# Norming h early into a second buffer, adaLN sections on VectorE, and three smaller edits to a four-layer trunk

## The chip, the core and the metric

The kernel runs on one core of a Trainium2 chip. The metric is the time of one execution on the device, in microseconds (us). Five engines work side by side and each takes its own instructions in order: TensorE (products; its weight loads are a queue of their own), VectorE, ScalarE, GpSimd, and SyncE, which issues nearly all DMAs.

## The reference

One inference step of a trunk of DEPTH = 4 layers over 384 tokens (128 context, 256 latent) of width 1024, in float32. Layer i mixes tokens by i mod 3: a chunked gMLP (layers 0 and 3), a pooling mixer (1), grouped-query attention (2). A gated ConvFFN follows in every layer. Each sub-layer norms, shifts and scales by adaLN, and adds a gated residual:

```python
m = silu(cond) @ w_ada[i] + b_ada[i]            # six sections: sh1, sc1, gt1, sh2, sc2, gt2
h = rms_norm(x, g_mix[i]) * (1 + sc1) + sh1
x = x + gt1 * mixer(h)
h = rms_norm(x, g_ffn[i]) * (1 + sc2) + sh2
a, u = split(h @ w_ffn_in[i])                   # 2 x 2816 wide
a = conv3(a) * conv_w + conv_b                  # width 3, along the tokens
x = x + gt2 * ((gelu(a) * u) @ w_ffn_out[i])
```

Context and latent tokens have a condition each, so each adaLN section is 1024 numbers for two conditions. The pooling mixer projects h in four groups and multiplies by a fixed 384-token averaging matrix.

## The kernel before

Features lie on partitions (8 blocks of 128, index k or d) and the 384 tokens along the free axis. `self.x` holds the residual stream, `hh` and `hl` the high and low part of h, 386 columns (TE) each: the two last columns carry the shift of the two conditions. A float32 product is made of three fp32r products (`mm3`): high weight by high h, low weight by high h, high weight by low h.

Weights stream through in chunks of 128x1024 in a written-out order (`chunk_plan`). SyncE loads a chunk into one of five `wraw` buffers. `w_split` makes `whi` on ScalarE (L338) and `wlo` on VectorE (L345), and `w_get` keeps three chunks split ahead of the one in use; there are four buffers of each part. AdaLN sections are chunks of the same stream, eight a section. The table `ADA` names for each phase which sections it makes and how: "ad" by `ada_dve` on VectorE (L380, two multiply-and-sum instructions a chunk), "ap" by `ada_pe` on TensorE (L398, four small products). `weave` lays them between the phase's weight chunks, leaving out a number of chunks at its head and tail (`EDGES`). `w_split` runs each "ad" chunk as soon as the weight chunk before it has been split.

A sub-layer's start works without the norm. While the residual is written (`residual`, L453), `prep` writes x times the gain into `hh`, `hl` and adds up the squares on the way (`square`); the first products of the next sub-layer begin at once. `stats` sums the squares over partitions with products of ones (L521), `diag` and `spread` (L536) lay the reciprocal root out as `rbs`, and the products' results are multiplied by it afterwards.

In `ffn` this goes: four `fr` chunks make f = 0 and 1 (block columns of `a` and `u`) into four PSUM banks, then `fi` makes f = 2 to 21 with two chunks and 48 products each, in two of six banks `mm`, and the epilogue of block f - 1 is issued inside block f. `epi_a` multiplies `a` and `u` by `rbs` on VectorE (L657, L661); `epi_b` adds the shift into `ab` on ScalarE (L671), scales (L673), and adds the two neighbours on VectorE (`ct`, L675); `epi_c` takes GELU (L681) and multiplies (`gg`, L684); `split_act` makes `gh` (L567) and `gl` (L568). `fo` is the second projection, in `out_proj`. `stat_k` is the k of `fr` before which the sums are made. In `gmlp` the phases are `gv`, `gu`, `go`; in `pool` a product of two rows (L948) brings in the shift's column sums before the averaging products, and the residual follows (L955).

## Time and profile before

| | |
|---|---|
| time, median of 3 runs | 1789.53 us (1789.23 to 1791.93) |
| the profiled execution: its own time | 1789.65 us |
| its span, first to last instruction | 1787.8 us |
| TensorE busy | 1766.3 us, 99% |
| VectorE busy | 1387.9 us, 78% |
| ScalarE busy | 873.9 us, 49% |
| read from memory | 308.06 MB |

The rows below come from that one execution. Times in them are counted from the span's start. PE is TensorE, PEld its weight loads, DVE VectorE, ACT ScalarE, POOL GpSimd, SP SyncE. A matmul's end is modelled, and consecutive ones overlap, so spacing is read from starts.

### The profile page before, as it was taken

How to read it: one execution, taken by the hardware profiler on the slowest of the kernel's cores; microseconds unless marked ns; L12 is line 12 of the kernel's file. 1: busy time of each engine (PE TensorE's matmuls, PEld its weight loads, DVE VectorE, ACT ScalarE, POOL GpSimd, SP SyncE). 2: the span in 40 equal slices, each digit the busy share in tenths (PEclk: the TensorE clock that was granted, in tenths of full speed). 3: DMA queues.
4: the chain of work that ended last, by engine and by line, in shares of the span. 5: the costliest groups of instructions: out<-in, count | busy, mean ns of one | idle time of the engine just before them, and what ended most of it. 6: DMA issues, size and time to landing. Idle time of an engine off the chain costs nothing.

```text
span 1787.8 us, 26990 instructions
## 1 busy us (share of the span) xinstructions
PE 1766.3 (99%) x10326; PEld 1682.8 (94%) x10326; DVE 1387.9 (78%) x2456; ACT 873.9 (49%) x1556; POOL 1.8 (0%) x30
## 2 busy tenths in 40 slices
PE   7999999999999999999999999999999999999999
PEld 5799899999998999999778999999988999999999
DVE  5877689998876888797787788878775787888732
ACT  3634335555445555432568465553354443555531
POOL 0000000000000000000000000000000000000000
PEclk9999999999999999999999999999999999999999
DMA  9775565554653444466543444436645255444341
GB/s 328 283 238 179 211 218 176 177 176 168 208 201 122 146 163 175 148 234 228 177 148 131 139 156 159 165 118 214 204 170 196 96 175 177 142 153 143 123 150 57
DMA packets 87637, 311.65 MB, mean 174 GB/s; under 512 B 10450, under 2 KB 10962, under 8 KB 87252
## 3 DMA queue, kind: packets, MB, share of 16 engines
q1 hardware_dynamic: 87364, 309.92, 49.8%
q8 instruction: 81, 1.33, 0.3%
q14 instruction: 48, 0.39, 0.1%
q10 hardware_dynamic: 144, 0.01, 0.0%
HBM read 308.06 MB, written 1.84 MB: 173 GB/s over the span
## 4 chain that ended last, share of the span: by engine, by line
PE 84%; DVE 10%; ACT 3%; issue 2%; DMA 1%; SPq 0%; DVEq 0%; ACTq 0%
PE mm L638 65%; PE mm L762 6%; DVE junk L380 3%; DVE wlo L345 2%; ACT whi L338 1%; PE S L638 1%; PE mm L806 1%; DMA wraw<-wts 1%; DVE ct L675 1%; PE S L1035 1%; PE psa L398 1%; PE adaT L638 1%; PE mm L928 1%; PE psa L762 1%; PE adaT L762 1%
## 5 line engine op out<-in xcount | busy, mean ns | idle before, releaser
L345 DVE TENSOR_TENSOR wlo<-wraw,whi 128x1024 fp32r<-128x1024 f32 (+2 forms) x390 | 465.8, 1200 | 188.7 <-ACT whi L338 187.7
L338 ACT ACTIVATE whi<-wraw 128x1024 fp32r<-128x1024 f32 (+2 forms) x390 | 399.7, 1035 | 305.3 <-PE mm L638 189.1
L638 PE MATMUL mm<-hh,whi 128*128 128x386 f32 (+1 forms) x1664 | 426.6, 341 | 0.0
L638 PE MATMUL mm<-hh,wlo 128*128 128x386 f32 (+1 forms) x1664 | 423.9, 340 | 0.7 <-DVE wlo L345 0.2
L638 PE MATMUL mm<-hl,whi 128*128 128x386 f32 (+1 forms) x1664 | 421.3, 338 | 0.0
L380 DVE SCALAR_TENSOR_TENSOR junk<-wraw,condb 128x1024 bf16<-128x1024 f32 x272 | 332.2, 1221 | 7.6 <-ACT condb L1499 2.7
L638 PEld LDWEIGHTS mm<-hh,whi 128*128 128x128 f32 x1664 | 300.6, 188 | 4.8 <-issue 2.1
L638 PEld LDWEIGHTS mm<-hh,wlo 128*128 128x128 f32 x1664 | 303.1, 188 | 2.0 <-DVE wlo L345 1.9
L638 PEld LDWEIGHTS mm<-hl,whi 128*128 128x128 f32 x1664 | 303.3, 188 | 0.0
L638 PE MATMUL mm<-gh,wlo 128*128 128x384 f32 x704 | 193.6, 336 | 0.0
L638 PE MATMUL mm<-gl,whi 128*128 128x384 f32 x704 | 193.6, 336 | 0.0
L638 PE MATMUL mm<-gh,whi 128*128 128x384 f32 x704 | 193.6, 336 | 0.0
L681 ACT ACTIVATE ct<-ct 128x385 f32<-128x385 f32 x88 | 46.1, 527 | 178.2 <-DVE ct L675 178.1
L638 PEld LDWEIGHTS mm<-gl,whi 128*128 128x128 f32 x704 | 128.5, 188 | 0.0
L638 PEld LDWEIGHTS mm<-gh,wlo 128*128 128x128 f32 x704 | 128.5, 188 | 0.0
L638 PEld LDWEIGHTS mm<-gh,whi 128*128 128x128 f32 x704 | 128.4, 188 | 0.0
L675 DVE SCALAR_TENSOR_TENSOR ct<-ab,par,ct 128x385 f32<-128x385 f32 x176 | 109.1, 621 | 22.3 <-ACT ct L673 17.4
L684 DVE SCALAR_TENSOR_TENSOR gg<-u,mm,ct 128x128 f32<-128x128 f32 (+1 forms) x176 | 66.3, 419 | 49.1 <-ACT ct L681 49.1
L586 ACT ACTIVATE hh<-x,A 128x128 fp32r<-128x128 f32 x96 | 43.2, 457 | 104.9 <-DVE x L453 94.1
L671 ACT ACTIVATE ab<-a,be 128x128 f32<-128x128 f32 (+1 forms) x176 | 70.7, 450 | 2.6
L657 DVE TENSOR_TENSOR a<-mm,rbs 128x384 f32<-128x384 f32 x88 | 48.6, 552 | 20.5 <-PE mm L638 14.5
L673 ACT ACTIVATE ct<-ab,par 128x385 f32<-128x385 f32 x88 | 62.7, 712 | 3.4
(301 smaller groups left out, 1961.9 us busy)
## 6 DMA issues: line engine op xcount, KB each, us to landing
wraw<-wts SPq DMA_DIRECT2D x562, 512.0 KB, 3.3
wraw<-wts SPq DMA_DIRECT2D x12, 256.0 KB, 2.6
wraw<-wts SPq DMA_DIRECT2D x8, 384.0 KB, 4.1
x<-x SPq DMA_DIRECT2D x4, 384.0 KB, 4.3
mx<-mix SPq DMA_DIRECT2D x1, 1280.0 KB, 7.1
y<-x SPq DMA_DIRECT2D x3, 384.0 KB, 3.1
condb<-condb SPq DMA_DIRECT2D x1, 1024.0 KB, 8.6
ws<-a_w_s SPq DMA_DIRECT2D x2, 512.0 KB, 4.0
```

What stands on the lines that cost most here:

```text
L338: nc.scalar.activation(hi[:, :n], t[:, :n], AF.Copy)
L345: nc.vector.tensor_tensor(out=lo[:, :n], in0=t[:, :n], in1=hi[:, :n].bitcast(F32), op=ALU.subtract)
L380: nc.vector.scalar_tensor_tensor(out=self.junk.bitcast(BF16), in0=w, scalar=1.0, in1=self.condb[:, c, :], op0=ALU.mult, op1=ALU.mult, accu ...
L586: nc.scalar.activation(self.hh[:, d, t0:t1], self.x[:, d, t0:t1], AF.Copy, scale=A[:, d, c:c + 1])
L638: nc.tensor.matmul(o, w[:, c:c + nw], r, start=(first and p == 0), stop=(last and p == 2))
L657: nc.vector.tensor_tensor(out=a1, in0=pa[:, 0:T], in1=rbs, op=ALU.mult)
L671: nc.scalar.activation(ab[:, p0:p1], a1[:, t0:t1], AF.Identity, bias=be[:, c:c + 1])
L673: nc.scalar.activation(t, ab[:, 1:T + 2], AF.Identity, scale=cw[1], bias=cb)
L675: nc.vector.scalar_tensor_tensor(out=t, in0=ab[:, i:i + T + 1], scalar=cw[i], in1=t, op0=ALU.mult, op1=ALU.add)
L681: nc.scalar.activation(t, t, GELU)
L684: nc.vector.scalar_tensor_tensor(out=g[:, t0:t1], in0=u1[:, t0:t1], scalar=bu[:, c:c + 1], in1=t[:, t0 + c:t1 + c], op0=ALU.add, op1=ALU.mult)
L762: nc.tensor.matmul(ps[n][i], hs, w[p == 1][:, c:c + 512], start=(k == 0 and p == 0), stop=(k == 7 and p == 2))
```

## The change

The second half of `ffn` reads a finished h. `norm` (with `put_act`) makes all eight blocks of h, normed, scaled and shifted, in a second buffer with rows of 384 columns as soon as `rbs` is known, and blocks f = 3 to 21 are made from it. Their epilogue needs no multiplication by `rbs` and no shift: ScalarE copies `a` from PSUM, takes GELU per group of tokens, and VectorE multiplies with `u` in PSUM. The sums are made and spread earlier (`stat_k`). From f = 2 to 7 the epilogue runs two blocks behind, at f = 8 two blocks are caught up. The two buffers `hb[0]` and `hb[1]` take turns; the idle one also holds the last eight blocks of `gh`, `gl` (or `ga`, `gb`, or the attention's `qS`). The gMLP's `gu` reads such plain rows too. `PLAIN`, `FPAD` and the pool `const2` only place buffers.

Three adaLN sections go from "ap" to "ad" (layer 0's fourth, layer 1's first, layer 2's third), and `ADA` and `EDGES` lay all sections out anew. At the start, products of ones (`warm`) stand before the first weights, before the first sums and after the first section. `add_square` adds the last square to the sum, so that `stats` takes one part. In `pool` the two rows of column sums are split into high and low parts at partitions 0, 32 and 64, so that one fp32r product takes the place of a float32 one.

The diff without its blank lines and a few lines of the same kind:

```diff
+NR = 3
+NG = NF - 8
+PLAIN = (32, 0)
+FPAD = 88
...
 ADA = {
-    (0, "gv"): [("ad", 0, 2)],
-    (0, "gu"): [("ad", 0, 3), ("ap", 0, 4)],
-    (0, "go"): [("ad", 0, 5), ("ap", 1, 1)],
-    (0, "fi"): [("ad", 1, 2), ("ad", 1, 0), ("ad", 1, 4, 0, 3)],
-    (0, "fo"): [("ad", 1, 4, 3, 8), ("ad", 1, 3)],
-    (1, "fi"): [("ad", 1, 5), ("ad", 2, 1, 0, 5)],
-    (1, "fo"): [("ad", 2, 1, 5, 8), ("ad", 2, 0), ("ad", 2, 4)],
-    (2, "nm"): [("ap", 2, 3, 0, 6)],
-    (2, "qkv"): [("ap", 2, 3, 6, 8)],
-    (2, "at"): [("ap", 2, 2), ("ap", 2, 5)],
-    (2, "fi"): [("ad", 3, 1), ("ad", 3, 2, 0, 3)],
-    (2, "fo"): [("ad", 3, 0), ("ad", 3, 2, 3, 8)],
-    (3, "gv"): [("ad", 3, 4), ("ad", 3, 3, 0, 1)],
-    (3, "go"): [("ad", 3, 3, 1, 8)],
+    (0, "gv"): [("ad", 0, 4)],
+    (0, "gu"): [("ad", 0, 2), ("ad", 0, 3, 0, 2)],
+    (0, "go"): [("ad", 0, 3, 2, 8), ("ad", 0, 5, 0, 3)],
+    (0, "fi"): [("ad", 0, 5, 3, 8), ("ad", 1, 1), ("ad", 1, 2), ("ad", 1, 0, 0, 5)],
+    (0, "fo"): [("ad", 1, 0, 5, 8), ("ad", 1, 4), ("ad", 1, 3)],
+    (1, "fi"): [("ad", 1, 5), ("ad", 2, 1), ("ad", 2, 0)],
+    (1, "fo"): [("ad", 2, 4), ("ad", 2, 3)],
+    (2, "nm"): [("ap", 2, 2, 0, 6)],
+    (2, "qkv"): [("ap", 2, 2, 6, 8)],
+    (2, "at"): [("ap", 2, 5)],
+    (2, "fi"): [("ad", 3, 1), ("ad", 3, 2)],
+    (2, "fo"): [("ad", 3, 0), ("ad", 3, 4, 0, 4)],
+    (3, "gv"): [("ad", 3, 4, 4, 8), ("ad", 3, 3, 0, 4)],
+    (3, "go"): [("ad", 3, 3, 4, 8)],
     (3, "fi"): [("ad", 3, 5)],
 }
-EDGES = {(0, "gv"): (2, 1), (0, "go"): (5, 0), (3, "gv"): (5, 2), "fi": (0, 6), (3, "go"): (5, 2)}
+EDGES = {(0, "gv"): (2, 1), (0, "go"): (5, 0), (3, "gv"): (5, 2), "fi": (8, 4), (3, "go"): (5, 2)}
...
+WARM = (25, 3, 10)
...
+        self.const2 = pool("const2", 1)
...
+    def add_square(self, pr):
+        self.nc.vector.tensor_tensor(out=pr["acc"], in0=pr["acc"], in1=pr["sq"], op=ALU.add)
...
+    def put_act(self, k, A, rbs, hi, lo, sh):
+        nc = self.nc
+        t = self.tmp.tile([128, T], F32, tag="sq", name="nt")
+        nc.vector.tensor_tensor(out=t, in0=self.x[:, k, :], in1=rbs, op=ALU.mult)
+        for c, (t0, t1) in enumerate(GRPS):
+            nc.scalar.activation(t[:, t0:t1], t[:, t0:t1], AF.Identity, scale=A[:, k, c:c + 1], bias=sh[:, k, c:c + 1])
+        nc.scalar.activation(hi[:, k, :], t, AF.Copy)
+        return lambda: nc.vector.tensor_tensor(out=lo[:, k, :], in0=t, in1=hi[:, k, :].bitcast(F32), op=ALU.subtract)
...
+    def use(self, n):
+        self.cur = n
+        w = KD * TE
+        self.hh, self.hl = (self.hb[n][:, w * i:w * i + w].rearrange("p (k t) -> p k t", t=TE) for i in range(2))
+    def plain(self, n):
+        w, o = KD * T, PLAIN[n]
+        return [self.hb[n][:, w * i + o:w * i + w + o].rearrange("p (k t) -> p k t", t=T) for i in range(2)]
...
     def ffn(self, l, pr, follow, stat_k):
         nc = self.nc
         hh, hl = self.hh[:, :, 0:TE], self.hl[:, :, 0:TE]
+        nh, nl = self.plain(1 - self.cur)
+        tail = self.plain(self.cur)
         with self.tc.tile_pool(name=f"ffn{l}", bufs=1) as fp:
-            gh = fp.tile([128, NF, T], F32R, tag="gh", name="gh")
-            gl = fp.tile([128, NF, T], F32R, tag="gl", name="gl")
+            fp.tile([128, FPAD], F32, tag="pad", name="pad")
+            own = [fp.tile([128, NG, T], F32R, tag=n, name=n) for n in ("gh", "gl")]
+            gh, gl = ([own[i][:, f, :] if f < NG else tail[i][:, f - NG, :] for f in range(NF)] for i in range(2))
...
             def epi_a(f, pa, pu):
+                if f >= NR:
+                    return f, pa, None, pu, None
...
                     p0, p1 = pos[c]
-                    nc.scalar.activation(ab[:, p0:p1], a1[:, t0:t1], AF.Identity, bias=be[:, c:c + 1])
+                    if f < NR:
+                        nc.scalar.activation(ab[:, p0:p1], a1[:, t0:t1], AF.Identity, bias=be[:, c:c + 1])
+                    else:
+                        nc.scalar.activation(ab[:, p0:p1], a1[:, t0:t1], AF.Copy)
...
             def epi_c(st, t):
-                _, _, _, u1, bu = st
+                f, _, _, u, bu = st
+                g = self.tmp.tile([128, T], F32, tag="gg", name="gg")
+                if f >= NR:
+                    for c, (t0, t1) in enumerate(GRPS):
+                        nc.scalar.activation(g[:, t0:t1], t[:, t0 + c:t1 + c], GELU)
+                    nc.vector.tensor_tensor(out=g, in0=u, in1=g, op=ALU.mult)
+                    return g
                 nc.scalar.activation(t, t, GELU)
-                g = self.tmp.tile([128, T], F32, tag="gg", name="gg")
                 for c, (t0, t1) in enumerate(GRPS):
-                    nc.vector.scalar_tensor_tensor(out=g[:, t0:t1], in0=u1[:, t0:t1], scalar=bu[:, c:c + 1],
+                    nc.vector.scalar_tensor_tensor(out=g[:, t0:t1], in0=u[:, t0:t1], scalar=bu[:, c:c + 1],
                                                    in1=t[:, t0 + c:t1 + c], op0=ALU.add, op1=ALU.mult)
                 return g
+            sh = self.prm[:, l, 24:32, :]
+            to_norm = list(range(KD))
+            def norm(n):
+                ks, to_norm[:] = to_norm[:n], to_norm[n:]
+                for i in range(0, len(ks), 2):
+                    for lo in [self.put_act(k, pr["A"], rbs, nh, nl, sh) for k in ks[i:i + 2]]:
+                        lo()
+            self.add_square(pr)
             b = [self.bank()[:, :TE] for _ in range(4)]
+            R = None
             for kk in range(4):
                 w = self.w_get("fr")
                 for k2 in range(2):
                     k = 2 * kk + k2
                     if k == stat_k:
-                        R = self.diag(self.stats(pr["acc"], pr["sq"]))
+                        R = self.diag(self.stats(pr["acc"]))
+                    if k == stat_k + 2:
+                        nc.scalar.activation(rbs, self.spread(R), AF.Copy)
+                        R = None
                     self.mm3([(b[i], 512 * k2 + 128 * i) for i in range(4)], w, (hh[:, k, :], hl[:, k, :]),
                              k == 0, k == 7)
-            nc.scalar.activation(rbs, self.spread(R), AF.Copy)
+                    if k > stat_k + 1:
+                        norm(2)
+            if R is not None:
+                nc.scalar.activation(rbs, self.spread(R), AF.Copy)
+            norm(2)
             prev = [(0, b[0], b[1]), (1, b[2], b[3])]
             for f in range(2, NF):
-                pa, pu = self.bank()[:, :TE], self.bank()[:, :TE]
+                w0 = TE if f < NR else T
+                pa, pu = self.bank()[:, :w0], self.bank()[:, :w0]
+                now, prev = (prev, []) if f == 8 else (prev[:1], prev[1:])
                 for kk in range(2):
                     if kk == 0:
                         sts = []
-                        w = self.w_get("fi", mid=lambda: sts.extend([epi_a(*p) for p in prev]))
+                        w = self.w_get("fi", mid=lambda: sts.extend([epi_a(*p) for p in now]))
                         ts = [epi_b(st) for st in sts]
                     else:
                         gs = [epi_c(st, t) for st, t in zip(sts, ts)]
                         w = self.w_get("fi")
                         for st, g in zip(sts, gs):
-                            self.split_act(g, gh[:, st[0], :], gl[:, st[0], :])
+                            self.split_act(g, gh[st[0]], gl[st[0]])
+                    if f < NR:
+                        norm(3)
                     for k4 in range(4):
                         k = 4 * kk + k4
-                        self.mm3([(pa, 256 * k4), (pu, 256 * k4 + 128)], w, (hh[:, k, :], hl[:, k, :]), k == 0, k == 7)
-                prev = [(f, pa, pu)]
+                        r = (hh[:, k, :], hl[:, k, :]) if f < NR else (nh[:, k, :], nl[:, k, :])
+                        self.mm3([(pa, 256 * k4), (pu, 256 * k4 + 128)], w, r, k == 0, k == 7)
+                prev.append((f, pa, pu))
+            assert not to_norm and len(prev) == 1
             sts = []
             self.w_split(self.n_get + 2, lambda: sts.extend([epi_a(*p) for p in prev]))
             g = epi_c(sts[0], epi_b(sts[0]))
-            self.split_act(g, gh[:, NF - 1, :], gl[:, NF - 1, :])
+            self.split_act(g, gh[NF - 1], gl[NF - 1])
+            self.use(1 - self.cur)
             res, after = follow()
...
+        hb = self.cur if pr is None else 1 - self.cur
+        vh, vl = self.plain(hb)
+        tail = self.plain(1 - hb)
         with self.tc.tile_pool(name=f"gmlp{l}", bufs=1) as gp:
             v = gp.tile([128, 3, DG], F32, tag="v", name="v")
-            ga = gp.tile([128, 16, T], F32R, tag="ga", name="ga")
-            gb = gp.tile([128, 16, T], F32R, tag="gb", name="gb")
+            own = [gp.tile([128, 8, T], F32R, tag=n, name=n) for n in ("ga", "gb")]
+            ga, gb = ([own[i][:, c, :] if c < 8 else tail[i][:, c - 8, :] for c in range(16)] for i in range(2))
...
+                self.add_square(pr)
...
-                            R = self.diag(self.stats(pr["acc"], pr["sq"]))
+                            R = self.diag(self.stats(pr["acc"]))
...
-                b = [self.bank()[:, :te] for _ in range(2)]
+                b = [self.bank()[:, :T] for _ in range(2)]
...
-                                 (self.hh[:, k, 0:te], self.hl[:, k, 0:te]), k == 0, k == 7)
+                                 (vh[:, k, :], vl[:, k, :]), k == 0, k == 7)
...
+            self.use(hb)
...
+            msr = pp.tile([128, 4, T], F32R, tag="msr", name="msr")
+            ush = pp.tile([128, 4, 256], F32R, tag="ush", name="ush")
+            nc.gpsimd.memset(msr.bitcast(F32), 0.0)
+            nc.gpsimd.memset(ush.bitcast(F32), 0.0)
...
-                u = pp.tile([128, 4, 256], F32, tag="u", name="u", bufs=3)
+                u = pp.tile([128, 3, 256], F32, tag="u", name="u", bufs=3)
+                if g == 0:
+                    for q in (0, 32):
+                        nc.vector.tensor_copy(msr[q:q + 2], ms)
+                    nc.vector.tensor_tensor(out=msr[64:66], in0=ms, in1=msr[0:2].bitcast(F32), op=ALU.subtract)
                 for i in range(3):
                     nc.scalar.activation(u[:, i, :], ps[i // 2][:, 256 * (i % 2):256 * (i % 2) + 256], AF.Copy,
                                          scale=r[:, i:i + 1])
-                nc.vector.tensor_copy(u[0:2, 3, :], ps[1][0:2, 256:512])
+                for q in (0, 64):
+                    nc.vector.tensor_copy(ush[q:q + 2, g, :], ps[1][0:2, 256:512])
+                nc.vector.tensor_tensor(out=ush[32:34, g, :], in0=ps[1][0:2, 256:512], in1=ush[0:2, g, :].bitcast(F32),
+                                        op=ALU.subtract)
...
-                    nc.tensor.matmul(ps, u[0:2, 3, c], ms[:, g, :], start=True, stop=False, skip_group_check=True)
+                    nc.tensor.matmul(ps, ush[:, g, c], msr[:, g, :], start=True, stop=False, skip_group_check=True)
...
-            qS = ap.tile([128, NH, T], F32R, tag="qS", name="qS")
+            o = PLAIN[1 - self.cur]
+            qS = self.hb[1 - self.cur][:, o:o + NH * T].rearrange("p (h t) -> p h t", t=T)
...
-        self.hh = self.const.tile([128, KD, TE], F32R, name="hh")
-        self.hl = self.const.tile([128, KD, TE], F32R, name="hl")
-        self.par = self.const.tile([128, NPAR], F32, name="par")
+        self.hb = [self.const.tile([128, 2 * KD * TE], F32R, name=f"hb{i}") for i in range(2)]
+        self.use(0)
+        self.par = self.const2.tile([128, NPAR], F32, name="par")
...
+        nc.scalar.activation(self.tmp.tile([128, 1], F32, tag="dmy", name="dmy", bufs=1), self.ones[:, 0:1], AF.Silu)
+        spare = self.bank("spare")
+        def warm(n):
+            for _ in range(WARM[n]):
+                nc.tensor.matmul(spare[:, 0:128], self.ones, self.ones, start=True, stop=True)
+        warm(0)
...
+        def first_stats():
+            warm(1)
+            r.append(self.stats(acc))
+        a0_mm(0, first_stats)
+        warm(2)
...
-            pr = self.ffn(l, pr, follow, 7 if kind == 1 else 5)
+            pr = self.ffn(l, pr, follow, 6 if kind == 1 else 3)
```

## Rows read from the trace of the kernel before

**Rows 1.** The page, busy time of each engine, share, instructions.
```profile
PE 1766.3 (99%) x10326; PEld 1682.8 (94%) x10326; DVE 1387.9 (78%) x2456; ACT 873.9 (49%) x1556; POOL 1.8 (0%) x30
```

**Rows 2.** Windows, L638 alone: layer 1's `fi`, layer 0's `fo`; busy (instructions).
```profile
590.00:750.00 160.00, 160.00 (x906) 160.00 (x906) 1.00 0.46 161
...
450.00:530.00 80.00, 80.00 (x463) 80.00 (x462) 1.00 0.60 208
```

**Rows 3.** Timeline, VectorE, layer 0's `fi`: start, duration, instruction [idle].
```profile
319.08 1.23 DVE L345 TENSOR_TENSOR wlo<-wraw,whi 128x1024 fp32r<-128x1024 f32 x1 [0.19 <-ACT whi L338]
320.22 0.55 DVE L568 TENSOR_TENSOR gl<-gg,gh 128x384 fp32r<-128x384 f32 x1
320.69 0.55 DVE L657 TENSOR_TENSOR a<-mm,rbs 128x384 f32<-128x384 f32 x1
...
321.62 1.21 DVE L345 TENSOR_TENSOR wlo<-wraw,whi 128x1024 fp32r<-128x1024 f32 x1
322.76 1.22 DVE L380 SCALAR_TENSOR_TENSOR junk<-wraw,condb 128x1024 bf16<-128x1024 f32 x1
...
325.17 1.27 DVE L675 SCALAR_TENSOR_TENSOR ct<-ab,par,ct 128x385 f32<-128x385 f32 x2
327.03 0.76 DVE L684 SCALAR_TENSOR_TENSOR gg<-u,mm,ct 128x128 f32<-128x128 f32 x2 [0.59 <-ACT ct L681]
327.98 1.22 DVE L345 TENSOR_TENSOR wlo<-wraw,whi 128x1024 fp32r<-128x1024 f32 x1 [0.19 <-ACT whi L338]
```

**Rows 4.** Timeline of TensorE: its first wait in that phase.
```profile
391.79 0.62 PE L638 MATMUL mm<-hh,wlo 128*128 128x386 f32 x2 [0.23 <-DVE wlo L345]
```

**Rows 5.** Timeline of TensorE around one adaLN chunk in layer 0's `gu`.
```profile
124.55 0.51 PE L638 MATMUL mm<-hl,whi 128*128 128x384 f32 x2
124.99 0.64 PE L398 MATMUL psa<-wraw,cond 128*32 128x256 f32 x8
125.56 0.62 PE L638 MATMUL mm<-hh,whi 128*128 128x384 f32 x2
```

**Rows 6.** Timeline of TensorE in layer 2's `fr`: one pair of sums, the spread.
```profile
1020.66 0.36 PE L521 MATMUL cs<-ones,sq 128*128 128x1 f32 x2
...
1027.32 0.81 PE L536 MATMUL adaT<-R,ones 128*128 128x384 f32 x2
```

**Rows 7.** Timeline of TensorE: adaLN products of the start.
```profile
9.38 1.08 PE L1437 MATMUL psa<-wraw,cond 128*32 128x256 f32 x8 [9.38 <-DMA wraw<-wts]
...
20.18 1.07 PE L1437 MATMUL psa<-wraw,cond 128*32 128x256 f32 x16
```

**Rows 8.** Timeline of the pool: column sums on TensorE, residual on VectorE.
```profile
560.73 0.91 PE L948 MATMUL mm<-ms,u 2*128 2x384 f32 x2
...
562.85 0.91 PE L948 MATMUL mm<-ms,u 2*128 2x384 f32 x2
...
562.02 0.73 DVE L955 SCALAR_TENSOR_TENSOR x<-mm,pgs,x 128x128 f32<-128x128 f32 x2
...
564.22 0.74 DVE L955 SCALAR_TENSOR_TENSOR x<-mm,pgs,x 128x128 f32<-128x128 f32 x2
```

**Rows 9.** Timeline of ScalarE in layer 0's `fi`.
```profile
321.48 0.81 ACT L671 ACTIVATE ab<-a,be 128x128 f32<-128x128 f32 x2
...
326.47 0.53 ACT L681 ACTIVATE ct<-ct 128x385 f32<-128x385 f32 x1 [3.44 <-DVE ct L675]
326.90 1.04 ACT L338 ACTIVATE whi<-wraw 128x1024 fp32r<-128x1024 f32 x1
327.85 0.51 ACT L567 ACTIVATE gh<-gg 128x384 fp32r<-128x384 f32 x1
```

**Rows 10.** Timelines of ScalarE and VectorE after layer 2's spread.
```profile
1028.16 0.49 ACT L697 ACTIVATE rbs<-adaT 128x384 f32<-128x384 f32 x1 [3.77 <-PE adaT L536]
...
1035.24 1.42 DVE L684 SCALAR_TENSOR_TENSOR gg<-u,mm,ct 128x128 f32<-128x128 f32 x4 [0.49 <-ACT ct L681]
```

**Rows 11.** Windows, the span's end: us, busy of five engines, granted clock.
```profile
1786.00:1788.00 2.00, 0.00 (x0) 0.00 (x0) 0.00 (x0) 0.00 (x0) 0.00 (x0) 0.70 0.20 73
```

41 lines of the change are left out of this document (19 added, 22 removed).

## The prediction

> **What bounds the kernel now.** First the busy totals [rows 1]: TensorE 99% of the span, VectorE 78%, ScalarE 49%. A busy TensorE is not yet TensorE at its best, so second I read the spacing of the products by stage [rows 2]. In layer 1's `fi` phase 906 products of 386 columns begin or end in 160 us, one every 176.6 ns; in layer 0's `fo` phase 463 of 384 columns in 80 us, one every 172.8 ns. Between the two stands no wait: over most of the span TensorE is simply supplied without gaps, and what is taken from it comes off the time one for one, as long as the others keep pace.
>
> Third I looked for the stage where they don't: VectorE's timeline over one block f of layer 0's `fi` [rows 3]. From the `wlo` at 319.08 to the one at 327.98 are 8.90 us: two `wlo` of 1.14, `gl` 0.47, `a` and `u` 0.93, one adaLN chunk 2.41 (322.76 to 325.17), two `ct` with the wait for GELU 1.86 (1.27 of work, 0.59 of wait), `gg` with the wait for the next `whi` 0.95. TensorE needs 48 x 176.6 = 8.48 us for the same f. So VectorE falls 0.42 us behind at each f, and its queue runs in order: both waits stay unfilled though it is late. TensorE notices only at 391.79 [rows 4], some 13 f after the phase settled at about 283 us. That is 13 x 0.42 = 5.5 us of cover, which the three chunks split ahead and the six banks give; I use 6. From there to the phase's end at 444 TensorE runs at VectorE's pace, about 5 f x 0.42 = 2 us lost.
>
> **The change part by part: what TensorE saves.** Narrower products: from f = 3 on `fi` reads h from a buffer with rows of 384 instead of 386 columns: 19 f x 48 = 912 products in each of four FFNs at 3.8 ns less is 13.9 us. Whether width or row pitch makes the 3.8 isn't settled by these rows; lower bound 0. A further 672 products in the gMLP's `gu` phases lose the pitch: 0 to 2.6, I take 2. The Trainium skill (TensorE: Matmul & The Clock Gate, "Wait — 56ns, not 53.3ns?") gives a warm product its columns at 2.4 GHz plus a small constant; two columns would then be 0.8 ns, the 13.9 would shrink to 3.0 and my sum below would end near 1822, but the trace shows 3.8 between its two kinds of rows.
>
> Three adaLN sections of eight chunks leave TensorE. From the pair of products before such a chunk to the next are 1.01 us [rows 5], where pairs otherwise follow each other by 0.35: 0.66 each. Sixteen lie in layer 0's `gu` and `go`, where TensorE is saturated: 10.6. Eight lie in the attention, where it also waits: 0 to 5.3, I take 2.6. The joined squares save half of the column sums in five places, 15 pairs of at most 0.36 us [rows 6], 3.3 to 5.4, I take 4; the added VectorE operation waits in a queue that stands idle there. At the start eight small products take 1.08 us at 9.38, while sixteen take 1.07 at 20.18 [rows 7]: TensorE is at half speed until then. Warming it with products of ones, while it waits for the first weights anyway, shortens the few products on the path up to 17 us, but the ten put behind the first section take some of it back: 0 to 3, I take 1.5. The pool's packed sums save at most 0.74 of the 0.91 us that each of eight such products takes, 6 us, but there VectorE needs 2.20 us for a block d (562.02 to 564.22) and TensorE 2.12 (560.73 to 562.85) [rows 8], and the change gives VectorE eleven small operations more; I take 0, between 6 saved and 6 lost. Moved allocations, list indexing, the earlier Silu table and the `gu` epilogue of layer 3 lie on idle time: 0. With the 2 us of layer 0's `fi` (its new stalls are counted in full below) the savings are 13.9 + 2 + 13.2 + 4 + 1.5 + 2 = 36.6 us.
>
> **What it adds: the block period on VectorE.** From f = 3 on `a` and `u` go (0.93). `gg` becomes shorter, but that gains nothing, since the next `wlo` waits for `whi`, and `whi` stands on ScalarE behind GELU. GELU becomes two calls; a pair of such calls takes 0.81 where one takes 0.53 [rows 9], which moves `whi` by 0.28. So a block with one adaLN chunk takes 8.90 - 0.93 + 0.28 = 8.25 us and one without 5.84, against TensorE's 48 x 172.8 = 8.29. Now the chunks: layer 0's `fi` gets 26 instead of 19, and `EDGES` (8, 4) lays them over 32 weight chunks, 16 blocks, where (0, 6) had laid them over 38. That is 1.63 a block, 5.84 + 3.92 = 9.76 us; layer 1 gets 24, 9.46 us; layer 2 gets 16, 8.25; layer 3 gets 8, 7.05. VectorE falls behind by 16 x 1.47 = 23.5 us in layer 0 and 16 x 1.17 = 18.7 in layer 1. Less a cover of 6 each: 17.5 + 12.7 = 30 us of waits on TensorE. With three whole chunks of cover (12.4) it would be 17, with none 42. Queued behind a late VectorE are the banks: from f = 3 to 7 the epilogue is two blocks behind, so all six banks are in use and the next block's first product waits for `gg`.
>
> **What it adds: the start of each FFN.** All eight h blocks are normed between the spread and f = 3. ScalarE gets `rbs` 0.84 us after the spread's start [rows 6, 10] and takes 0.49. Then come four pairs: product with `rbs` 0.55, two activations with scale and bias plus one copy on ScalarE (0.81 + 0.51 [rows 9], up to 1.6 if two operands cost extra), the second block's the same, subtraction 0.55. The next pair's product stands behind that subtraction in VectorE's queue, so a pair is 3.5 to 4.1 us, I take 3.8, and a chunk's split (1.04 and 1.2) falls between the first two: 17 us. Only then does block 0's epilogue begin: `a`, `u`, `wlo`, `ct`, GELU, `gg`, about 5 us. So `gg` of block 0 ends 1.3 + 17 + 5 = 23.3 us after the spread. TensorE by then has done three k of 2.1 and f = 2 in 8.5, 15 to 15.5 us, and stands: f = 3 needs the banks of block 0. In the kernel before this is met just in time, `gg` of both blocks at 1035.24 to 1036.66 [rows 10]. The stall is 8 us by this; I take 7 in each FFN, 28 in all. With VectorE's own work as the only limit (eight times 1.02) it would be 0.3 each, with slow pairs 8.8. Layer 1, which norms later, ends alike: GELU and `gg` of block 0 stand behind five of its eight blocks.
>
> **The sum.** 1789.65 (the profiled execution's own time, 0.12 above the median) - 36.6 + 30 + 28 = 1811 us.
>
> **The rivals.** (1) VectorE keeps pace, and the change is faster. If the waits for ScalarE inside a block were filled (1.35 of the 9.76), layer 0 would need 8.41, which the cover absorbs, and the norming 8.2 us at each start. Both stalls go: 1789.65 - 36.6 = 1753, up to 1765 with remnants. It decides at a block period of 8.3 to 8.7 in layer 0's `fi`. For it: VectorE's bare work fits. Against it: the waits in [rows 3], which stay open though VectorE is late.
>
> (2) Only one of the two stalls is real: 1781 or 1783, 0.4% faster; with remnants of the other no change.
>
> (3) The stalls also slow the clock. Behind the last product the granted clock's mean falls to 0.70 in a stretch of 2 us [rows 11], and at the start TensorE ran at half speed from 9.38 until after 17 us. If each of the four stalls at an FFN's start did that, the next products would cost up to 4 us more each: 1819 to 1827. The Trainium skill (TensorE: Matmul & The Clock Gate, "What's actually happening") names these levels as 1.2 and 2.4 GHz and says that an idle engine falls back to the lower one; the end of this trace agrees.
>
> **How the numbers follow.** My forecast, both stalls at the full clock, 1795 to 1822, has 0.48: each half rests on a count in the code and a duration in a row, but the new epilogue's period is not in the trace. Rival 1 has 0.22, rival 2 0.16, rival 3 0.14. The range reaches into rivals 1 and 3, leaving out about a tenth on either side: 1760 to 1832; the forecast's own is 1795 to 1822. A measurement of this kernel tells 0.2% (3.6 us) from no change. Faster: rival 1 and most of rival 2, 0.32. The same: what is left of rival 2 and of the forecast's lower edge, 0.06. Slower: 0.62.
>
> **What would show it.** In layer 0's `fi` blocks of over 9 us on TensorE, released by `wlo` or `gg`, against 8.3 in layer 3's. A gap on TensorE of some 7 us, 15 us after the spread of each FFN, released by `gg`. Products of `fi` at the spacing of `fo`. No small adaLN products in layer 0. The prediction is wrong if VectorE shows a block period under 8.5 us with three chunks in two blocks, or if block 0's `gg` comes before f = 2 ends.

## The result and the profile after

The changed kernel takes 1842.92 us in the median of 4 runs (1841.15 to 1845.00); beside it the kernel before took 1789.74. The ratio is 1.0297, 95% interval 1.0284 to 1.0309: slower by 53 us, where 21 were forecast. It lies 10.9 us above the top of the range.

The page of the profiled execution (1842.56 us): busy totals against [rows 1], and TensorE's granted clock in 40 slices.

```profile
span 1840.7 us, 26758 instructions
PE 1757.1 (95%) x10166; PEld 1683.3 (91%) x10166; DVE 1392.4 (76%) x2380; ACT 885.5 (48%) x1638; POOL 4.0 (0%) x32
PEclk9999999999999899999999989999999999899999
```

TensorE has 9 us less to do and the span is 53 longer: it waits. The waits view says for whom (total, times, longest):

```profile
PE mm L675 <- DVE gg L736: 27.9, 7, 8.7
PE mm L675 <- ACT be L703: 13.1, 3, 4.4
PE mm L675 <- ACT whi L349: 9.7, 8, 3.6
PE mm L675 <- DVE wlo L356: 7.0, 11, 0.8
PE mm L1042 <- DVE ush L1032: 6.4, 3, 3.6
```

The first two are the starts of the four FFNs, with 2.8 of the 27.9 at block 5 of layers 0 and 1; the next two the late blocks of layers 0 and 1 and the end of layer 0's `fo`; the last is the pool. A further 4.8 in three waits is for `gg` (L732) at blocks 7 and 8 of layers 0 and 1. By stages, from the starts of TensorE's products in both traces:

| stage | before | after | difference | forecast |
|---|---|---|---|---|
| start to layer 0's `fr` | 252.77 | 239.42 | -13.4 | -13.1 |
| layer 0 `fi` | 171.88 | 192.47 | +20.6 | +19 |
| layer 0 `fo` | 91.68 | 98.89 | +7.2 | 0 |
| pool | 29.27 | 31.14 | +1.9 | 0 |
| layer 1 `fi` | 170.16 | 194.66 | +24.5 | +16 |
| attention | 163.67 | 162.02 | -1.7 | -2.6 |
| layer 2 `fi` | 170.16 | 178.32 | +8.2 | +3.5 |
| layer 3 `fi` | 170.16 | 178.07 | +7.9 | +3.5 |

Inside `fi`, the pitch of the blocks (start of block f to start of f + 1, f = 2 to 21; 8.79 once and then 8.49 throughout in layers 1 to 3 of the kernel before):

```
layer 0  13.04 14.76  8.32  9.92 8.32 10.17 10.47 8.32 8.32 8.32 8.32 8.32 9.30 9.19 10.68 9.34 9.20 10.48 9.35 8.32
layer 1   8.76 19.53 14.76  9.98 8.32  9.96  8.32 8.32 8.32 8.32 8.32 8.32 9.05 9.39  9.34 9.22 9.34  9.42 9.35 8.32
layer 2  13.04 15.52  8.32 (18 times)
layer 3  13.03 15.28  8.32 (18 times)
```

So there are two things to see in each `fi`: two very long blocks at its start, in every layer, and in layers 0 and 1 later blocks of 9 to 11, first at blocks 5 to 8, where TensorE waits for banks, then from block 14 on, where it waits for split weights. Over the flat 8.32 the long ones cost 11.2, 18.1, 11.9 and 11.7 us, 52.9 in all, and the others 14.9 in layer 0 and 10.2 in layer 1.

The start of layer 2's `fi`, TensorE's timeline (start, duration, instruction, count, wait ahead of it and who ended it):

```profile
1058.04 0.81 PE L551 MATMUL adaT<-R,ones 128*128 128x384 f32 x2
...
1073.23 0.52 PE L675 MATMUL mm<-hb,whi 128*128 128x386 f32 x2
1078.13 0.45 PE L675 MATMUL mm<-hb,whi 128*128 128x384 f32 x1 [4.38 <-ACT be L703]
1082.60 0.66 PE L675 MATMUL mm<-hb,whi 128*128 128x384 f32 x1 [4.03 <-DVE gg L736]
...
1083.70 1.48 PE L675 MATMUL mm<-hb,whi 128*128 128x384 f32 x4
...
1090.19 0.86 PE L675 MATMUL mm<-hb,whi 128*128 128x384 f32 x4
```

In layer 1, whose sums come later, TensorE waits in block 3 and again in block 4:

```profile
616.21 0.66 PE L675 MATMUL mm<-hb,whi 128*128 128x384 f32 x1 [8.72 <-DVE gg L736]
...
631.90 0.66 PE L675 MATMUL mm<-hb,whi 128*128 128x384 f32 x1 [4.87 <-DVE gg L736]
```

What VectorE did in layer 2 meanwhile:

```profile
1059.40 1.03 DVE L584 TENSOR_TENSOR nt<-x,rbs 128x384 f32<-128x384 f32 x2 [0.93 <-ACT rbs L759]
1061.58 0.56 DVE L588 TENSOR_TENSOR hb<-nt,hb 128x384 fp32r<-128x384 f32 x1 [1.14 <-ACT hb L587]
...
1069.18 1.02 DVE L584 TENSOR_TENSOR nt<-x,rbs 128x384 f32<-128x384 f32 x2
...
1073.26 1.02 DVE L584 TENSOR_TENSOR nt<-x,rbs 128x384 f32<-128x384 f32 x2
...
1077.32 0.55 DVE L701 TENSOR_TENSOR a<-mm,rbs 128x384 f32<-128x384 f32 x1
...
1081.70 0.76 DVE L736 SCALAR_TENSOR_TENSOR gg<-u,mm,ct 128x128 f32<-128x128 f32 x2 [0.59 <-ACT ct L734]
```

Four norm pairs, the last two 4.08 apart (1069.18 to 1073.26), stand in VectorE's queue ahead of block 0's `a` at 1077.32. `gg` of block 0 ends at 1082.46, 24.4 us after the spread began; TensorE had nothing left to do 15.7 after it. It stands for 4.38 + 4.03 = 8.4 us. That is the wait the prediction drew, 23.3 and 15 to 15.5. What came on top is in the next rows: four products take 1.48 where later four take 0.86. The windows of this stretch (us, busy of PE, PEld, DVE, ACT, POOL with instructions, granted clock, DMA share, GB/s) show the granted clock:

```profile
1066.00:1074.00 8.00, 7.75 (x44) 7.42 (x42) 3.96 (x9) 5.68 (x13) 0.00 (x0) 1.00 0.19 66
1074.00:1079.00 5.00, 0.45 (x1) 0.19 (x1) 2.99 (x6) 4.67 (x10) 0.00 (x0) 0.95 0.00 0
1079.00:1090.00 11.00, 7.40 (x26) 7.43 (x27) 9.68 (x16) 6.51 (x10) 0.00 (x0) 0.56 0.45 147
```

Full before and during most of the wait, 0.56 on the mean behind it: nearly nine tenths of these 11 us at the lower of TensorE's two levels, 1.2 instead of 2.4 GHz. The two blocks are 28.56 - 16.64 = 11.9 too long: 8.4 of it is wait, and most of the other 3.5 the slower clock (block 2's wider rows are 0.2).

### The profile page after: what moved, and what is told of

It reads as the page before. It is cut to its first block, busy times and chain, and to the rows that moved or that the text cites. A ratio compares the mean times of both kernels' runs of the same rounds, so it can differ in the third digit from the quotient of the medians.

```text
span 1840.7 us, 26758 instructions
## 1 busy us (share of the span) xinstructions
PE 1757.1 (95%) x10166; PEld 1683.3 (91%) x10166; DVE 1392.4 (76%) x2380; ACT 885.5 (48%) x1638; POOL 4.0 (0%) x32
## 4 chain that ended last, share of the span: by engine, by line
PE 64%; DVE 21%; ACT 10%; issue 4%; DMA 2%; DVEq 0%; SPq 0%; ACTq 0%
PE mm L675 50%; DVE junk L391 7%; DVE wlo L356 6%; PE mm L841 5%; ACT whi L349 3%; DVE ct L722 3%; ACT nt L586 2%; DMA wraw<-wts 1%; PE S L675 1%; PE mm L885 1%; ACT hb L587 1%; DVE gl L593 1%; ACT gg L731 1%; PE adaT L675 1%; PE S L1130 1%
## 5 line engine op out<-in xcount | busy, mean ns | idle before, releaser
L675 PE MATMUL mm<-hb,whi 128*128 128x384 f32 (+1 forms) x4064 | 898.3, 340 | 52.0 <-DVE gg L736 27.9
L675 PEld LDWEIGHTS mm<-hb,whi 128*128 128x128 f32 x4064 | 727.6, 190 | 60.0 <-issue 30.1
L675 PE MATMUL mm<-hb,wlo 128*128 128x384 f32 (+1 forms) x2032 | 525.1, 339 | 5.6 <-DVE wlo L356 5.6
L391 DVE SCALAR_TENSOR_TENSOR junk<-wraw,condb 128x1024 bf16<-128x1024 f32 x320 | 391.1, 1222 | 8.4 <-ACT condb L1610 2.7
L675 PEld LDWEIGHTS mm<-hb,wlo 128*128 128x128 f32 x2032 | 371.8, 190 | 8.5 <-DVE wlo L356 8.5
L675 PE MATMUL mm<-gh,whi 128*128 128x384 f32 x448 | 123.8, 337 | 3.6 <-ACT whi L349 3.6
L675 PE MATMUL mm<-gh,wlo 128*128 128x384 f32 x448 | 124.0, 338 | 1.4 <-DVE wlo L356 1.4
L675 PE MATMUL mm<-gl,whi 128*128 128x384 f32 x448 | 123.8, 337 | 0.0
L841 PE MATMUL mm<-whi,hb 128*128 128x512 f32 x320 | 86.7, 396 | 0.1
L732 DVE TENSOR_TENSOR gg<-mm,gg 128x384 f32<-128x384 f32 x76 | 42.4, 558 | 47.4 <-ACT gg L731 46.7
L841 PEld LDWEIGHTS mm<-whi,hb 128*128 128x128 f32 x320 | 59.9, 187 | 15.5 <-ACT v L848 0.6
```

Source lines behind the costliest of these rows:

```text
L391: nc.vector.scalar_tensor_tensor(out=self.junk.bitcast(BF16), in0=w, scalar=1.0, in1=self.condb[:, c, :], op0=ALU.mult, op1=ALU.mult, accu ...
L675: nc.tensor.matmul(o, w[:, c:c + nw], r, start=(first and p == 0), stop=(last and p == 2))
L732: nc.vector.tensor_tensor(out=g, in0=u, in1=g, op=ALU.mult)
L841: nc.tensor.matmul(ps[n][i], hs, w[p == 1][:, c:c + 512], start=(k == 0 and p == 0), stop=(k == 7 and p == 2))
```

## The experiments

Sixteen kernels ran. Those that undo or change one thing come first, then the repairs. Theory A at the outset: three causes that add up, the FFN starts (block 0's epilogue behind the norm), VectorE's block period in layers 0 and 1, and layer 0's `fo`. Rival: the sections alone make VectorE late, at the starts too.

**The two large edits, each undone and both.** `k1_table` takes `ADA` and `EDGES` from the kernel before. `k2_late` takes the early norm out:

```diff
-NR = 3
+NR = NF
-            to_norm = list(range(KD))
+            to_norm = []
-                now, prev = (prev, []) if f == 8 else (prev[:1], prev[1:])
+                now, prev = prev, []
-            self.use(1 - self.cur)
```

(with `stat_k`, the spread and the place of `gh`'s tail to match). `k3_both` has both diffs.

> The changed kernel with the old placement of the adaLN sections (both tables from the kernel before). Theory A, three separate causes (VectorE's period in the blocks of layers 0 and 1, layer 0's fo with its 19 chunks, and the waits at each feed-forward start): the late blocks of fi in layers 0 and 1 fall back to the pitch of 8.32 and layer 0's fo to 91.7, together some 14.9 + 6.5 + 7.2 = 29 less; TensorE's adaLN comes back in layer 0's gu and go, and in the attention, some 12 more; the start of each fi keeps its two long blocks. About 1826 (1820 to 1832). Rival, the sections alone: VectorE is late at the starts too only because of the sections that it was given, and the starts lose their waits as well: about 1780 to 1785.

> The changed kernel without the early norm: all blocks read the 386-column h with the epilogue of before, the new placement of the sections stays. Theory A: the waits at the start of each fi go (about 11 in layers 0, 2 and 3, 18 in layer 1, some 51 in all); the narrower products and the short epilogue go with them, 17 x 0.17 x 4 = 12 more, and layers 0 and 1 have VectorE as bound with a longer period, 10 to 20 more than now: about 1815 to 1825, with the blocks of layers 2 and 3 flat at 8.49. Rival, the sections alone: the starts wait because of the sections, and this kernel is no faster than the changed one, 1840 to 1860.

> The changed kernel without the early norm and with the old placement of the sections: what is left is the products of ones, the joined squares, the packed column sums and gu's rows without the two extra columns. Theory A: faster than the kernel before by the joined squares (prediction: 4), the start (1.5) and gu's pitch (2), less 2 for the pool: 1780 to 1786. Rival, the second buffer itself costs (its place in memory, its row pitch): 1790 or above.

| median, us | sections as before | sections moved |
|---|---|---|
| h normed late | 1790.27 (`k3_both`) | 1834.50 (`k2_late`) |
| h normed early | 1834.49 (`k1_table`) | 1842.92 (changed kernel) |

(Ratios to the kernel before: 0.9998, 0.9989 to 1.0007, for `k3_both`; 1.0245 and 1.0246 for the other two.) Each edit alone costs 44 us, both together 53. Neither theory said that. The rival falls: without the moved sections the starts still have their long blocks, 14.88 and 17.16 in layer 0, even longer: with the old `EDGES` of (0, 6) one adaLN chunk stands on VectorE ahead of the norm pairs and one inside block 0's epilogue, 2.4 us each. The causes of A are seen, but they don't add up. With the old sections layer 0's later blocks are flat at 8.32 and its `fo` takes 91.69; with the early norm undone layer 2's blocks are flat at 8.52. But under the moved sections the long epilogue of the late norm makes the later blocks of layers 0 and 1 worse than the short one does: some 25 and 19 us over its flat 8.52, against 14.9 and 10.2, with blocks up to 11.5 (`fi` 195.3 and 189.9 in all), and 104.9 for layer 0's `fo`, 96.5 for layer 1's. So the early norm pays back there most of what it costs at the starts: 19 in the later blocks, 11 in the two `fo`, and 13 by the narrower products.

`k3_both` came out at 1790.3, not at 1780 to 1786. Its stages: `fr` 0.6 to 0.7 shorter, but the pool 32.75 instead of 29.27. Two kernels of one small edit on the kernel before settle that, `k7_packed` with the pool's packed sums, `k14_squares` with `add_square` and one part in `stats`.

> The kernel before with one edit alone, the packed column sums of the pool. The prediction gave it 0, 6 either way. Theory A: the three short copies on VectorE for each group stand ahead of the product that needs them, TensorE waits for them, and the pool is longer by what the kernel with both large edits undone showed, 32.7 against 29.3: about 1793 (1791.5 to 1795). Rival, the eight products fewer decide: 3 less, 1786 to 1788.

> The kernel before with one edit alone, the joined squares: one VectorE addition in place of a second set of column sums on TensorE, at five places. The prediction took 4. Theory from the kernel with both large edits undone: fr 0.6 to 0.7 shorter four times and the gMLP of layer 3 0.3: about 3 less, 1787 (1785.5 to 1788.5). Rival, the addition delays the statistics by as much: 1789.8.

`k7_packed`: 1794.06, ratio 1.0024 (1.0015 to 1.0032), 4.2 us slower. Its waits view and VectorE's timeline in the pool:

```profile
PE mm L959 <- DVE ush L949: 7.1, 3, 3.6
```

```profile
541.70 1.93 DVE L942 CAST msr<-ms 2x1536 fp32r<-2x1536 f32 x2 [1.09 <-DMA ms<-mixsum]
543.66 1.75 DVE L943 TENSOR_TENSOR msr<-ms,msr 2x1536 fp32r<-2x1536 f32 x1
545.44 0.86 DVE L948 CAST ush<-mm 2x256 fp32r<-2x256 f32 x2
546.33 0.41 DVE L949 TENSOR_TENSOR ush<-mm,ush 2x256 fp32r<-2x256 f32 x1
```

Splitting and placing the two rows takes VectorE 5 us before the first packed product can go, and the averaging products stand behind that product; the eight halved products don't give this back. `k14_squares`: 1786.22, ratio 0.9983 (0.9974 to 0.9992), 3.5 faster. The two nearly cancel, and that is why `k3_both` shows nothing.

**What the long blocks wait for.** `k4_nr5` sets `NR = 5`, so that the normed h is needed two blocks later.

> The changed kernel with NR = 5: blocks 3 and 4 read the 386-column h too, so the normed h is needed 17 us later, in the same order of work. If TensorE waits at block 3 for the banks of block 0, whose epilogue stands behind the norm on VectorE and ScalarE: the waits stay, and the two wider blocks add 2 x 0.17 x 4 = 1.4: 1842 to 1848. Rival, it waits for the normed rows themselves: the waits at the starts go, some 40 less: about 1800.

1848.05 (1.0315, 1.0298 to 1.0333): the waits stay, in layer 2 at 13.03 and 14.38, and TensorE's total wait for `gg` is

```profile
PE mm L675 <- DVE gg L736: 34.3, 12, 8.7
```

so it is the banks, not the normed rows.

**The clock.** `k6_ones` puts products of ones, into a bank that is free, ahead of block 3:

```diff
+                    if (f, kk) == (3, 0):
+                        spare = self.ps_bank()
+                        for _ in range(56 if l == 1 else 32):
+                            nc.tensor.matmul(spare[:, 0:128], self.ones, self.ones, start=True, stop=True)
```

> The changed kernel with products of ones on TensorE ahead of block 3 in each layer (32 of them, 56 in layer 1), into a bank that nothing else uses there, so that TensorE works through its wait. Theory A, the clock is a cost of its own: the waits stay as long as they were, the stretches at half clock behind them go, about 3 each: 1843 - 12 = 1831 (1827 to 1836). Rival, the fall of the clock is hidden by VectorE being the bound there (the next wait gets shorter by as much): 1840 to 1845.

1840.01 (1.0281, 1.0267 to 1.0295), against 1.0297 (1.0284 to 1.0309): the intervals overlap, and the time is the rival's. The traces tell more. Layer 3 in the changed kernel, then in this one, windows as above:

```profile
1575.00:1582.00 7.00, 1.71 (x7) 0.98 (x5) 4.68 (x8) 5.55 (x13) 0.00 (x0) 0.87 0.00 0
1582.00:1592.00 10.00, 7.13 (x26) 7.17 (x27) 7.76 (x13) 6.61 (x11) 0.00 (x0) 0.58 0.47 159
```

```profile
1574.00:1584.00 10.00, 8.91 (x74) 8.66 (x73) 6.38 (x12) 8.40 (x16) 0.00 (x0) 1.00 0.15 54
1584.00:1590.00 6.00, 5.56 (x32) 5.59 (x33) 5.29 (x8) 3.60 (x8) 0.00 (x0) 1.00 0.35 115
```

The clock stays up, and layer 3's two long blocks take 25.73 instead of 28.31, 2.6 less. In layers 0 and 1 that comes back: their `fi` takes 192.4 and 196.3 instead of 192.5 and 194.7, since VectorE is the bound there and the next wait grows. So the half clock is a real cost, worth 1.6 us in layer 2 (`fi` 176.7 instead of 178.3) and 2.6 in layer 3, but only where VectorE has room; the forecast of 12 less for all four was too much by far.

**Another order.** `k5_order` puts block 0's epilogue first and spreads the norm over the next blocks, without touching the sections:

```diff
-NR = 3
+NR = 5
-                    if k > stat_k + 1:
-                        norm(2)
-            norm(2)
-                    if f < NR:
-                        norm(3)
+                    norm({(2, 1): 2, (3, 0): 2, (3, 1): 2, (4, 0): 2}.get((f, kk), 0))
```

> The changed kernel with the order of the feed-forward start changed: no norm in fr, block 0's epilogue first, then a pair of the norm in each half of blocks 2, 3 and the first half of 4, with NR = 5 so that block 5 is the first to read the normed h. Theory A (the waits at the starts come from block 0's epilogue standing behind the norm): the two long blocks at each start go, some 42 to 48 less, the wider blocks add 2: about 1798 (1792 to 1806); what is left over the kernel before are the late blocks and the fo of layer 0 and the late blocks of layer 1. Rival, the norm's own load on VectorE and ScalarE is what makes them late, wherever it stands: the waits come back in blocks 4 to 7, less than half is won, 1820 to 1840.

1853.98 (1.0358, 1.0342 to 1.0374), slower still. Theory A's repair fell: blocks 2 and 3 are now flat, and blocks 4 and 5 take 16.37 and 14.96 in layer 2. TensorE there, then VectorE ahead of the first wait's end:

```profile
1090.50 0.66 PE L675 MATMUL mm<-hb,whi 128*128 128x386 f32 x1 [4.97 <-DVE gg L736]
...
1106.80 0.66 PE L675 MATMUL mm<-hb,whi 128*128 128x384 f32 x1 [4.90 <-DVE gg L736]
```

```profile
1083.12 1.22 DVE L391 SCALAR_TENSOR_TENSOR junk<-wraw,condb 128x1024 bf16<-128x1024 f32 x1
...
1085.54 1.02 DVE L584 TENSOR_TENSOR nt<-x,rbs 128x384 f32<-128x384 f32 x2
1087.70 0.56 DVE L588 TENSOR_TENSOR hb<-nt,hb 128x384 fp32r<-128x384 f32 x1 [1.14 <-ACT hb L587]
1089.13 0.56 DVE L588 TENSOR_TENSOR hb<-nt,hb 128x384 fp32r<-128x384 f32 x1 [0.87 <-ACT hb L587]
1089.61 0.75 DVE L736 SCALAR_TENSOR_TENSOR gg<-u,mm,ct 128x128 f32<-128x128 f32 x2
```

`gg` of block 1 stands behind a norm pair and an adaLN chunk. That gave theory B: two blocks behind, an epilogue has no period to spare. `k9_lag` is this kernel with the epilogue one block behind from the start (`now, prev = prev, []`).

> The kernel with the changed start order and one edit more: each block's epilogue is done in the next block from the first on, as in the kernel before (both pending ones in block 2), and not one block later until block 8. Theory B, which takes the place of A: with the epilogue two blocks behind, the six banks are all in use, and whatever stands ahead of an epilogue's last reader on VectorE or ScalarE (norm pair, adaLN part) goes straight into TensorE's wait; one block behind there is a period to spare. The two long blocks at each start go, some 13 to 18 each, 55 to 62 in all: 1854 - 58 = 1796 (1790 to 1806). Rival, the engines have too much to do in the first blocks in either order: the waits come back in blocks 5 to 8, less than half is won, 1825 to 1845.

1842.21 (1.0298, 1.0281 to 1.0315), 12 less than `k5_order` and not 58. The banks are no longer waited for; one long block is left, block 5 (14.4 to 19.1). It waits for the normed rows, four times and 11.4 in all, and in layers 0 to 2 for split weights too. Theory C moved their first reader once more: `k13_nr6` is `k9_lag` with `NR = 6`.

> The kernel with the epilogue one block behind and the sections of the changed kernel, with NR = 6 in place of 5, one size alone. Theory C: layers 2 and 3 lose the long block 5, 7.5 and 6 less, with 0.2 more each for the wider block; layers 0 and 1 win little, since VectorE is the bound through their whole fi (every block there is above 8.32) and what the start gives comes back as later waits: 1842 - 14 = 1828 (1822 to 1834). Rival, the wait is for banks still: no change, 1842.

1844.80 (1.0330, 1.0291 to 1.0369): C fell too. Block 5 is hardly shorter (13.2 to 18.7), block 6 is longer (10.9 to 12.1), and the wait has another name, the split weights:

```profile
1610.42 1.01 PE L675 MATMUL mm<-hb,whi 128*128 128x384 f32 x2 [4.27 <-ACT whi L349]
```

```profile
1606.04 0.99 ACT L586 ACTIVATE nt<-nt,prm,A 128x128 f32<-128x128 f32 x2 [3.91 <-DVE nt L584]
...
1608.49 0.52 ACT L587 ACTIVATE hb<-nt 128x384 fp32r<-128x384 f32 x1
1608.92 0.51 ACT L734 ACTIVATE ct<-ct 128x385 f32<-128x385 f32 x1
1609.33 1.04 ACT L349 ACTIVATE whi<-wraw 128x1024 fp32r<-128x1024 f32 x1
```

That `whi` stands on ScalarE behind the last norm pair, which waited 3.91 us for VectorE. Three repairs, and each time most of the wait only moved to the next thing made by the late engine: banks, normed rows, weights. In kind that is what the rivals of `k5_order` and `k9_lag` had said, too much work in the first blocks in either order.

**With fewer sections.** Three kernels went the same way with the packed sums taken out and fewer chunks: `k8_mend` is `k5_order` with a table between the two, `k10_mend2` the same with the epilogue one block behind, `k12_best` has `NR = 6` and the old `ADA` with `EDGES` (6, 2) for `fi`.

> The order of the kernel with the changed start, without the packed column sums, and with a table between the two: layer 0's section 4 and layer 2's section 3 on VectorE, layer 1's section 1 back on TensorE in layer 0's go, 20 sections' parts in the fi of layers 0 and 1, 13 in layer 0's fo. Theory A, each cause has its own repair: start 8 less than before, narrower products and short epilogue 17 x 4 x 0.17 = 12 less, squares 3 less, attention 2 less: 1766 (1760 to 1774). Rival, the early norm costs what the narrower products give back: 1780 or above.

> The mended kernel (table between the two, no packed column sums, changed start order) with the epilogue one block behind from the first on, and one adaLN part moved from layer 1's fo to its fi. Theory B: the long blocks go as above, layer 1's fo falls by 2 to 4: 1836 - 62 = 1774 (1766 to 1782). Rival (too much work in the first blocks): 1800 to 1820.

> The kernel with the epilogue one block behind, without the packed column sums, with NR = 6 and the sections placed as in the kernel before (in fi from the seventh weight chunk on). Theory C: the long block that was left at block 5 waits for the last pair of the norm, which stands behind the epilogues; with block 6 as the first to read the normed h it has one period more and the wait goes. By stages: start 252, fr 4 x 18.3, fi 4 x 167.5, fo 4 x 91.7, pool 29.3, attention 163.2, gMLP of layer 3 214, and some 5 around: 1777 (1773 to 1783). Rival, VectorE and ScalarE have too much work in the first blocks in any order, so that the wait goes on to block 6 or 7: 1792 to 1805.

They gave 1836.21 (1.0258, 1.0244 to 1.0272), 1816.45 (1.0149, 1.0134 to 1.0164) and 1808.20 (1.0102, 1.0089 to 1.0116). All three stayed above their forecasts, mainly by what the long blocks 4 to 6 kept, 6 to 17 us in each layer. `k11_late2` tried the sections from the other side: late norm, no packed sums, and one section alone moved to VectorE (layer 0's section 4, counted from 0), so that `gu` and `go` hold twelve adaLN chunks each on VectorE.

> The kernel with both large edits undone, without the packed column sums, and with one section alone moved to VectorE (layer 0's section 4, in layer 0's gv, gu and go, where VectorE has room): the kernel at 1790.3 less 3.5 for the pool and 5.3 for TensorE's section: 1781.5 (1778 to 1785). Rival, VectorE is the bound in gu and go too: 1787 or above.

1787.60 (0.9989, 0.9979 to 0.9998). The pool gave its share, the section nothing: TensorE now waits in `go` (1.75 us for `whi`, 0.73 for `wlo`) where it had none of this. In the changed kernel `go` holds nine chunks and no stall.

**The idle time inside the norm.** Theory D: VectorE is late as a whole in the first blocks, and half of each pair is idle time, spent waiting for ScalarE. `k15_put` is `k12_best` with the norm in the attention's form (`put`: two multiplications by gain and `rbs` and two subtractions a block on VectorE, no wait between), one pair behind each epilogue:

```diff
-                    for lo in [self.put_act(k, pr["A"], rbs, nh, nl, sh) for k in ks[i:i + 2]]:
-                        lo()
+                    self.put(ks[i:i + 2], lambda k: pr["A"][:, k, :], rbs, nh, nl, l, 24)
-                    norm({(2, 1): 2, (3, 0): 2, (3, 1): 2, (4, 0): 2}.get((f, kk), 0))
+                    norm(2 if f < NR and kk else 0)
```

and `EDGES` (8, 2) for layer 0's `fi`, (10, 2) for the others. `k16_nr7` is the same with `NR = 7`.

> Theory C fell: the long block is still at block 5, and it waits for the split weights, whose ScalarE copy stands behind the last norm pair. Theory D: VectorE is late as a whole, by the sum of the work and of the waits of its queue in the first blocks (a pair of the norm takes 4.1 there, half of it idle while ScalarE works), and the wait shows wherever the slack ends. This kernel is the one with all mends, with the norm in the form that the attention uses (more work on VectorE, less on ScalarE, no idle time between, about 2.7 a pair), one pair behind each block's epilogue in blocks 2 to 5, and the adaLN parts from the ninth or eleventh weight chunk on. Theory D: four pairs 5.5 shorter and no adaLN part among them leave VectorE ahead, no block above 9: 1777 (1772 to 1784). Rival, it is the number of steps and not the idle time: 1790 to 1808.

> The kernel before this one with NR = 7, one size alone. Its waits on TensorE in fi are four, one in each layer, 12.7 in all, each for the first half of the last normed row, at block 6, the first narrow one. Theory D: with block 7 as the first narrow one they go: blocks at 8.5 and 8.32 throughout, 4 x 167.4, some 17 less and 1 more for the wider blocks: 1776 (1773 to 1780). Rival, as at the earlier mends the wait only goes to the next thing that is late (banks or split weights): 1787 to 1792.

`k15_put`: 1791.63 (1.0008, 0.9999 to 1.0017), 16.6 less than `k12_best` but above theory D's range; the number is the rival's. The form of the norm, its places and `EDGES` changed together, so how much of the 16.6 is the idle time is not shown. In its trace TensorE has one long block a layer left, and this is all it waits for in `fi`:

```profile
PE mm L675 <- ACT hb L573: 12.7, 4, 5.3
```

`k16_nr7`: 1784.54 (0.9973, 0.9964 to 0.9983), faster than both kernels, by 5.1 us against the one before. Those waits are gone; its page, and what is left in `fi`:

```profile
PE 1764.2 (99%) x10372; PEld 1678.9 (94%) x10372; DVE 1355.9 (76%) x2385; ACT 871.1 (49%) x1609; POOL 1.8 (0%) x30
PEclk9999999999999999999999999999999999999999
```

```profile
PE mm L675 <- DVE wlo L356: 4.9, 8, 1.2
PE mm L675 <- ACT whi L349: 1.0, 1, 1.0
```

It fell short of 1776 by layer 0, where `fi` takes 175.0: VectorE has nearly one adaLN chunk a block there on top of the norm. Layers 1 to 3 take 170.1, 168.0 and 167.4, against 170.16 before. Of the 5.1 us the joined squares account for 3.5 by themselves, and the two intervals overlap (0.9964 to 0.9983, 0.9974 to 0.9992). So with its costs repaired the early norm is worth some 2 us by this, and that it gains at all is not shown. Putting it into layers 2 and 3 alone was not tried.

## Why the prediction was wrong

The direction was right, and so were the two mechanisms that it priced, the block period and the wait for block 0's banks. One term was much too small, one was left out without a reason, and one taken at nothing cost a little; the sum came out 31.6 us short of the profiled execution.

**The savings** were about right. Products: layer 3's 48 now take 8.32 us instead of 8.49, 173.3 ns instead of 176.9, 12.9 us over the 19 blocks of four layers for 13.9 forecast. The rule of the Trainium skill (TensorE: Matmul & The Clock Gate, "Wait — 56ns, not 53.3ns?") would have given 0.8 ns a product; the measured 3.6 decides against the 1822 that hung on it. Start with `gu` and `go`: -13.4 for -13.1 (10.6, 1.5 and half of the 2 for `gu`). Squares 3.5 for 4. The attention gained 1.7, not 2.6.

**The block period** was right. VectorE in layer 0, timeline from one `wlo` to the next but one, with two adaLN chunks in it:

```profile
382.35 1.23 DVE L356 TENSOR_TENSOR wlo<-wraw,whi 128x1024 fp32r<-128x1024 f32 x1 [0.40 <-ACT whi L349]
...
391.88 0.56 DVE L732 TENSOR_TENSOR gg<-mm,gg 128x384 f32<-128x384 f32 x1 [0.69 <-ACT gg L731]
392.83 1.23 DVE L356 TENSOR_TENSOR wlo<-wraw,whi 128x1024 fp32r<-128x1024 f32 x1 [0.39 <-ACT whi L349]
```

10.48 us; 5.84 + 2 x 2.41 is 10.66. It costs 14.9 and 10.2 for 17.5 and 12.7, the waits for banks at blocks 5 to 8 included, and the waits for ScalarE inside a block stayed open, as said against rival 1.

**The step that failed is the size of the FFN start**, "I take 7 in each FFN, 28 in all"; it is 52.9. In layers 0, 2 and 3 the wait itself was 8.2 to 8.4, the 8 that had been worked out and lowered to 7 without a reason. What came on top, 3.0 to 3.5 and most of it the half clock, had been left to rival 3 with 0.14, though [rows 11] showed the clock falling within 4 us of the last product (it ends at 1784.2). The forecast should have held it. In layer 1 "ends alike" was wrong: its sums come at k = 6, so the spread comes behind all of `fr`, and TensorE has the 8.8 us of block 2 left and not 15. It waits 8.72 and 4.87 and loses 18.1. Of the 24.9 that are missing, 10.3 are wait (38.3 instead of 28, 6.6 of it in layer 1) and 14.6 came on top of the waits. The run with products of ones shows that not all of these 14.6 can be had back: in layers 0 and 1 the next wait took it.

**Layer 0's `fo` was costed at nothing.** It got 19 chunks where the kernel before had 13, behind a `fi` that ended late. VectorE runs them ahead of the residual, and the next weights' split on ScalarE stands behind the residual's `hb`: TensorE waits 3.56 at 534.95, 0.82 at 536.20 and 0.62 at 509.61, 5.0 of the 7.2, and behind them the granted clock is 0.84 on the mean from 534 to 545. ScalarE's wait for the residual, and TensorE's:

```profile
529.60 0.90 ACT L611 ACTIVATE hb<-x,A 128x128 fp32r<-128x128 f32 x2 [5.21 <-DVE x L464]
534.95 0.44 PE L675 MATMUL mm<-gh,whi 128*128 128x384 f32 x1 [3.56 <-ACT whi L349]
```

In `k1_table`, with 13 chunks and no late blocks in `fi`, the 7.2 are gone; which of the two does it was not separated. **The pool** was 0 with 6 either way; the edit costs 4.2 alone and showed 1.9 here, inside the 6.

Starts +24.9, `fo` +7.2, pool +1.9, block period -4.9: 29.1 of the 31.6; the rest is the small shortfalls among the savings.

## What to carry to other kernels

Work that is added ahead of the last reader of a PSUM bank is to be priced not by its busy time but by its length in the in-order queue, waits for the other engine included (here 4.1 us a pair, half of it idle). Reordering alone moved most of the wait to the next thing that the late engine makes. It ended when the pairs had no idle time, stood one behind each epilogue, had the adaLN chunks later and one block more of slack; which of these was needed is open. Two edits that load the same engine are to be priced together, since each can hide or pay the other's cost (44 and 44 gave 53 here). And when a stall on TensorE of several microseconds is forecast, the slower clock behind it belongs in the forecast, not in a rival.
